# The general path's weight loads, issued from GpSimd's queue in place of ACT's

## The chip, the cores and the metric

One core of a Trainium2 chip runs the whole kernel. The metric is the device time of one execution in microseconds (us); lower is better. The core has five engines with a queue of instructions each: TensorE (PE; PEld is its weight load), VectorE (DVE), ScalarE (ACT), GpSimd (POOL) and SyncE (SP). Each queue runs in its own order, and a queue waits for another through semaphores.

## The reference, cut to what matters

Two layers, each a mixer (pooling, a recurrent scan in both directions, attention, an output product, LayerNorm) and then a mixture of experts over 256 tokens. Of the 32 experts every token uses two, and the result goes through a LayerNorm:

```python
def expert_block(args):
    xb, e = args
    h = jax.nn.silu(xb @ w_gate[e]) * (xb @ w_up[e])
    return h @ w_down[e]
...
x = layer_norm(DEEPNORM_ALPHA * x + m, ln2_g[l], ln2_b[l])
```

The weights of all 32 experts are read in each layer, whatever the tokens choose: three matrices of 1024 x 512 in float32 for each.

## The kernel before, in words

**The fast path.** Each layer's experts run in NQ = 8 quarters of four experts (the loop over q in `experts`). Every expert has CH = 32 slots for tokens. A quarter gathers its tokens by products with a one-hot matrix (`gather_steps`, the helper at L168), scales them into the tiles xg on ACT (`gathered`, L1230), multiplies by the gate and up weights (`gate_up`; all its products are issued by the helper at L172 and go by the tiles pg and pu), transposes the result, multiplies by the down weights (`down`, tile py) and adds the gated result to the tokens (`combine`, tile pc).

**The weights.** A quarter has 24 weight slabs of 1 MiB (128 partitions x 2048 floats), 192 in a layer. They are loaded by SP alone, in order, by the generator `loads` at L1039, into a ring of RING = 22 slabs. The program is unrolled, and each time a quarter takes a slab, the next load is put into SP's queue, so the queue runs FLIGHT = 22 slabs ahead. A load must wait until the slab that it writes over has been read by TensorE.

**Completion semaphores.** The framework counts the loads of SP's and ACT's queues on eight semaphores that the two queues share, taken in turn. Before each load SP waits until the load eight places earlier has landed (the EVENT_SEMAPHORE instructions at L1039), so at most eight are in flight.

**The general path.** An expert that is chosen by more than 32 tokens needs further passes. After the second quarter (q equal to OVQ = 1) `overflow` reads the largest slot count on all five queues (`values_load`, L1304) and branches (`tc.If(cv > CH)`, L1305). Inside are two nested loops at run time, which load weights in pieces of 256 KiB into the tiles ow on ACT's queue (`piece`, L1317): 24 x 4 = 96 loads in one pass of the body. POOL computes nothing inside.

When the branch isn't taken, each queue runs the else side that the framework adds. It brings every semaphore that the body would have counted up to the value that the body would have left, so that what follows the branch can wait for one value. In the program of the kernel before, the else side holds one such instruction for ACT, for PE and for DVE, none for POOL, and eight for SP, one for each shared semaphore. Each first waits for the count that stands for all loads issued so far, and then adds the body's share:

```text
else side, SP, for each of the eight shared DMA semaphores:
    wait until the semaphore is at least 192, then add 192      (96 loads / 8 semaphores x 16)
```

The xg tiles behind the branch lie in the same ring of buffers as ow (tag "r", 9 buffers), so the first ACT instruction behind the branch (L1230) waits for these semaphores. Of the 24 slabs of a quarter, 22 can lie in the ring.

Of the kernel before, what the change touches and what calls it, by code (L numbers as in the profile page):

```python
# [68 lines left out]
def tile_encoder(ctx: ExitStack, tc: tile.TileContext, x_tok, x_t, w_a0, w_a1, w_b0, w_b1, w_o,  # L69
                 cols, ln_rows, consts, rcnt, e_w, out):  # L70
    nc = tc.nc
# [137 lines left out]
    def s2(shape, name):  # L209
        return mp.tile(shape, F32, name=name, tag="r", bufs=RB)  # L210
# [987 lines left out]
    def one_hot(slots):  # L1198
        oh = s1([128, 2, 4, CH], "OH")
        io = iota[:, 0:CH].rearrange("p (a b s) -> p a b s", a=1, b=1).to_broadcast([128, 2, 4, CH])  # L1200
        V.tensor_tensor(oh, io, slots.rearrange("p i (a s) -> p i a s", s=1).to_broadcast([128, 2, 4, CH]), op=OP.is_equal)  # L1201
        return oh
# [6 lines left out]
    def experts(l, x1, xr, oh0, exps, gates, count, wts, feed):  # L1209
# [24 lines left out]
        def gather(oh):  # L1234
            banks = None
            for banks in gather_steps(oh):
                pass
            return gathered(banks)

        def gated(oh, gts):  # L1240
            V.tensor_tensor(oh, oh, gts.rearrange("p i (a s) -> p i a s", s=1).to_broadcast([128, 2, 4, CH]), op=OP.mult)

        def slots_t(oh):
            pt = bank("oht")
            for i in range(2):
                PE.transpose(pt[:, 128 * i:128 * i + 128], oh[:, i].rearrange("p a s -> p (a s)"), ident)  # L1246
            oht = s1([128, T], "OHT")
            A.copy(oht, pt[:, 0:T])
            return oht

        def gate_up(xg, w, between=lambda n: None):
            ps_g, ps_u = bankc("pg"), bankc("pu")
            for m, ps in enumerate((ps_g, ps_u)):
                for k in range(8):
                    wk_ = w(8 * m + k)
                    for a in range(4):
                        mm(ps[quad(a)], xg[k // 4][:, k % 4, CH * a:CH * a + CH], wk_(a), start=(k == 0), stop=(k == 7))
                    between(8 * m + k)
            h_ = s2([128, 512], "h")
            A.activation(h_, ps_g, AF.Silu)  # L1260
            V.tensor_mul(h_, h_, ps_u)  # L1261
            return h_

        def hid_t(h_):
            h3 = h_.rearrange("p (c k) -> p k c", k=4)
            pt = bank("pht")
            for k in range(4):
                PE.transpose(pt[:, 128 * k:128 * k + 128], h3[:, k], ident)
            hT = s2([128, 4, 128], "hT")
            V.tensor_copy(hT, pt.rearrange("p (k s) -> p k s", k=4))  # L1270
            return hT

        def down(hT, w, between=lambda n: None, keep=None):
            y = []
            if keep is not None:
                keep["y"] = y
            for hf in range(2):
                py = bank("py")
                for k in range(4):
                    wk_ = w(16 + 4 * hf + k)  # L1280
                    for a in range(4):
                        mm(py[quad(a)], hT[:, k, CH * a:CH * a + CH], wk_(a), start=(k == 0), stop=(k == 3))
                    between(4 * hf + k)
                y_ = s2([128, 512], "y")
                A.copy(y_, py)  # L1285
                y.append(y_)
            return y
# [7 lines left out]
        def combine_all(oht, y):  # L1295
            for hf in range(2):
                for i in range(2):
                    combine(oht, y, hf, i)
# [4 lines left out]
        def overflow():  # L1303
            cv = nc.values_load(cnt[0:1, 0:1], min_val=0, max_val=T)  # L1304
            with tc.If(cv > CH):  # L1305
                ovf = s2([128, 3, 2, NE], "ovf")
                sl, gt, tmp = (ovf[:, m] for m in range(3))
                V.tensor_copy(sl, slot)
                V.tensor_copy(gt, gate)
                with tc.For_i(0, T // CH - 1, 1):  # L1310
                    V.tensor_scalar(sl, sl, float(CH), None, op0=OP.subtract)
                    with tc.For_i(0, NQ, 1) as qi:
                        def wt(n):
                            def piece(a):
                                t_ = s2([128, 512], "ow")
                                v_ = e_w[l, :, n][bass.ds(qi, 1)].rearrange("o p n -> (o p) n")
                                nc.scalar.dma_start(out=t_, in_=v_[:, 512 * a:512 * a + 512])  # L1317
                                return t_
                            return piece

                        oh = one_hot(sl[:, :, 0:4])
                        xg = gather(oh)
                        gated(oh, gt[:, :, 0:4])
                        oht = slots_t(oh)
                        combine_all(oht, down(hid_t(gate_up(xg, wt)), wt))
                        for z in (sl, gt):
                            V.tensor_copy(tmp[:, :, 0:NE - 4], z[:, :, 4:NE])
                            V.tensor_copy(tmp[:, :, NE - 4:NE], z[:, :, 0:4])
                            V.tensor_copy(z, tmp)
# [307 lines left out]
```

## Time and profile before

| | us |
|---|---|
| median of 3 runs | 1278.93 |
| lowest, highest | 1277.48, 1283.57 |
| profiled execution, its own time | 1281.9 |
| span of the profiled execution | 1280.1 |

The span runs from the first to the last instruction of one profiled execution; its own time lies 1.8 us above the span and 3.0 us above the median of the runs. TensorE is busy for 77% of the span, DVE for 26%, ACT for 19%, POOL for 7%; the mean granted clock of TensorE is 0.871. The core moves 438.67 MB at a mean of 343 GB/s. SP's loads go over the hardware queue q1, ACT's over q10.

In the rows below a name such as SPq or ACTq is the queue of that engine, that is, instructions that its sequencer handles alone (branches, semaphores, DMA issues).

### The profile page before, as it was taken

The page shows a single profiled execution, that of the slowest core. Times are in us where ns is not written, and L with a number is a line of the kernel's source. Part 1 is how long each engine was busy: PE and PEld are TensorE (multiplying, and loading weights), DVE is VectorE, ACT ScalarE, POOL GpSimd, SP SyncE. Part 2 cuts the span into 40 slices and gives each one's busy share as a digit, 9 for nine tenths or more (in the row PEclk, how much of TensorE's full clock was granted, in tenths as well). Part 3 has the DMA queues.
Part 4 walks back from the last instruction along what each step waited for, and adds up shares of the span by engine and source line. Part 5 has one row for each costly group of instructions (what it writes and reads, how often), then busy time and mean ns, then how long its engine had stood idle before and what let it go on. Part 6 is the DMA issues. An engine that isn't in the chain of part 4 may idle for free. (4 is left out here: it accounts for less than half of the span.)

```text
span 1280.1 us, 18020 instructions
## 1 busy us (share of the span) xinstructions
PE 985.9 (77%) x7571; PEld 480.6 (38%) x7571; DVE 335.9 (26%) x774; ACT 239.2 (19%) x554; POOL 94.0 (7%) x137
## 2 busy tenths in 40 slices
PE   8988998933997777776698979989239977777753
PEld 7755763220441212221286657632214422223100
DVE  5937632110100001010368286411001000010103
ACT  5326422001110101010252353220011101010000
POOL 1143000000000000000101451000000000000002
PEclk9979999965998888886799789999669988888887
DMA  9413789998999999999940227999989999999994
GB/s 373 165 37 131 307 327 418 420 418 331 420 419 419 420 420 420 420 419 420 417 170 9 89 79 320 365 420 420 419 330 420 419 420 420 419 420 420 419 420 188
DMA packets 63452, 438.67 MB, mean 343 GB/s; under 512 B 7040, under 2 KB 7296, under 8 KB 11520
## 3 DMA queue, kind: packets, MB, share of 16 engines
q1 hardware_dynamic: 62784, 436.61, 83.1%
q8 instruction: 64, 1.05, 0.3%
q10 hardware_dynamic: 576, 0.79, 0.2%
q14 instruction: 28, 0.23, 0.0%
HBM read 436.32 MB, written 1.05 MB: 342 GB/s over the span
## 5 line engine op out<-in xcount | busy, mean ns | idle before, releaser
L172 PE MATMUL pg<-w,xg 128*32 128x512 f32 x1024 | 143.4, 658 | 120.3 <-ACT xg L1230 73.1
L172 PE MATMUL pu<-w,xg 128*32 128x512 f32 x1024 | 157.0, 700 | 39.2 <-DMA w<-in_e_w_dram 39.1
L172 PE MATMUL py<-w,hT 128*32 128x512 f32 x1024 | 146.0, 697 | 53.4 <-DMA w<-in_e_w_dram 42.4
L1261 DVE TENSOR_TENSOR h<-h,pu 128x512 f32<-128x512 f32 x16 | 11.0, 688 | 422.5 <-PE pu L172 218.3
L172 PEld LDWEIGHTS pg<-w,xg 128*32 128x32 f32 x1024 | 25.3, 114 | 215.8 <-DMA w<-in_e_w_dram 87.2
L1230 ACT ACTIVATE xg<-xg,lnc 128x128 f32<-128x128 f32 x112 | 41.8, 457 | 326.5 <-PE xg L168 219.6
L1293 DVE TENSOR_TENSOR xr<-xr,pc 128x512 f32<-128x512 f32 x56 | 38.5, 688 | 242.2 <-PE pc L172 242.2
L168 PEld LDWEIGHTS xg<-OH,xr 128*128 128x128 f32 x256 | 65.0, 331 | 61.9 <-issue 55.5
L168 PEld LDWEIGHTS xg<-OH,x 128*128 128x128 f32 x256 | 65.0, 331 | 59.4 <-issue 53.0
L172 PEld LDWEIGHTS py<-w,hT 128*32 128x32 f32 x1024 | 29.1, 117 | 154.1 <-DMA w<-in_e_w_dram 83.4
L168 PE MATMUL xg<-OH,xr 128*128 128x128 f32 x256 | 75.7, 433 | 12.0 <-DVE OH L1201 4.0
L168 PE MATMUL xg<-OH,x 128*128 128x128 f32 x256 | 75.6, 429 | 11.0 <-PEq L1305 4.1
L172 PE MATMUL pc<-y,OHT 128*128 128x512 f32 x128 | 70.0, 641 | 1.4 <-ACT y L1285 1.4
L1285 ACT COPY y<-py 128x512 f32<-128x512 f32 x32 | 18.7, 585 | 242.8 <-PE py L172 242.8
L231 POOL TENSOR_TENSOR w<-w 128x512 fp32r<-128x512 f32 (+1 forms) x20 | 25.2, 1265 | 497.4 <-ACT w L230 497.4
L172 PEld LDWEIGHTS pu<-w,xg 128*32 128x32 f32 x1024 | 23.6, 116 | 97.7 <-DMA w<-in_e_w_dram 80.5
L269 PE MATMUL wo<-w 128*128 128x512 f32 x192 | 46.5, 398 | 0.0
L196 POOL TENSOR_TENSOR lnmv<-lnmv,eps 128x1 f32<-128x1 f32 x8 | 4.8, 602 | 524.5 <-DVE lnmv L195 524.5
L172 PEld LDWEIGHTS pc<-y,OHT 128*128 128x128 f32 x128 | 20.1, 190 | 54.4 <-issue 46.0
L269 PEld LDWEIGHTS wo<-w 128*128 128x128 f32 x192 | 35.6, 188 | 9.1 <-issue 1.6
L230 ACT CAST w<-w 128x512 fp32r<-128x512 f32 (+1 forms) x64 | 36.6, 602 | 8.8 <-DMA w<-in_w_a_dram 4.8
L168 PE MATMUL pq<-w 128*128 128x512 f32 x64 | 38.0, 740 | 0.0
(328 smaller groups left out, 1064.8 us busy)
## 6 DMA issues: line engine op xcount, KB each, us to landing
w<-in_e_w_dram SPq DMA_DIRECT2D x384, 1024.0 KB, 19.9
w<-in_w_b_dram SPq DMA_DIRECT2D x8, 1024.0 KB, 18.7
w<-in_w_o_dram SPq DMA_DIRECT2D x8, 1024.0 KB, 19.9
w<-in_w_a_dram SPq DMA_DIRECT2D x4, 1024.0 KB, 13.5
lnr<-in_ln_rows_dram SPq DMA_DIRECT2D x12, 256.0 KB, 14.5
w<-in_w_a_dram SPq DMA_DIRECT2D x4, 448.0 KB, 6.3
w<-in_w_a_dram SPq DMA_DIRECT2D x2, 896.0 KB, 12.4
w<-in_cols_dram SPq DMA_DIRECT2D x2, 790.0 KB, 10.5
```

What stands on the lines that cost most here:

```text
L168: PE.matmul(ps, lhsT=lhsT, rhs=rhs, start=start, stop=True, skip_group_check=True)
L172: PE.matmul(ps, lhsT=lhsT, rhs=rhs, start=start, stop=stop)
L196: G.tensor_tensor(mv[:, 3:4], mv[:, 2:3], eps[:, 4:5], op=OP.pow)
L230: A.copy(hi, src)
L231: (V, G)[LOW[m]].tensor_tensor(lo, src, hi.bitcast(F32), op=OP.subtract)
L269: PE.matmul(ps, lhsT=l_[a], rhs=r_[b], start=first and n == 0, stop=last, skip_group_check=True)
L1230: A.activation(t_[:, k], ps[:, k], AF.Identity, scale=lnc["g1"][:, m:m + 1], bias=lnc["b1"][:, m:m + 1])
L1261: V.tensor_mul(h_, h_, ps_u)
L1285: A.copy(y_, py)
L1293: V.tensor_add(o_, o_, ps)
```

## The change

The loads of the general path are issued by GpSimd's queue. Nothing else differs: tiles, sizes, order and the branch are those of before.

```diff
@@ -1314,7 +1314,7 @@
                             def piece(a):
                                 t_ = s2([128, 512], "ow")
                                 v_ = e_w[l, :, n][bass.ds(qi, 1)].rearrange("o p n -> (o p) n")
-                                nc.scalar.dma_start(out=t_, in_=v_[:, 512 * a:512 * a + 512])
+                                nc.gpsimd.dma_start(out=t_, in_=v_[:, 512 * a:512 * a + 512])
                                 return t_
                             return piece
```

## Rows read from the trace of the kernel before

**Rows 1.** Page, part 2: GB/s moved in 40 slices of 32 us.
```profile
GB/s 373 165 37 131 307 327 418 420 418 331 420 419 419 420 420 420 420 419 420 417 170 9 89 79 320 365 420 420 419 330 420 419 420 420 419 420 420 419 420 188
```

**Rows 2.** The chain that ended last: start us, us, what.
```profile
947.95 0.47 ACT xg L1230
...
956.50 12.64 DMA w<-in_e_w_dram
...
969.20 19.90 DMA w<-in_e_w_dram
...
1250.07 12.58 DMA w<-in_e_w_dram
```

**Rows 3.** DMA issues by line and queue: KB each, us to landing.
```profile
q10 hardware_dynamic: 576, 0.79, 0.2%
...
w<-in_rcnt_dram ACTq DMA_DIRECT2D x2, 256.0 KB, 2.7
...
out_dram<-xr ACTq DMA_DIRECT2D x1, 160.0 KB, 2.3
out_dram<-xr ACTq DMA_DIRECT2D x1, 96.0 KB, 1.7
```

**Rows 4.** Line L1305, the branch: duration ns min/median/max, first and last start us.
```profile
L1305 SPq EVENT_SEMAPHORE  x16: 17/17/17, 291.8 to 947.8; - x16
L1305 POOLq COMPARE_BRANCH  x2: 45/45/45, 218.2 to 856.1; - x2
L1305 ACTq COMPARE_BRANCH  x2: 45/50/54, 256.1 to 894.1; - x2
L1305 PEldq COMPARE_BRANCH  x2: 6012/6050/6088, 256.8 to 894.8; - x2
...
L1305 ACTq EVENT_SEMAPHORE  x2: 17/17/17, 261.4 to 899.4; - x2
L1305 PEldq EVENT_SEMAPHORE  x2: 51/51/51, 262.9 to 900.8; - x2
L1305 SPq COMPARE_BRANCH  x2: 50/52/53, 290.5 to 928.8; - x2
```

**Rows 5.** The same line from 255 to 320 us, the first layer's branch alone.
```profile
L1305 SPq EVENT_SEMAPHORE  x8: 17/17/17, 291.8 to 309.2; - x8
```

**Rows 6.** Waits, who for whom: us in total, times, longest.
```profile
ACT xg L1230 <- SPq L1305: 106.9, 2, 53.7
...
SPq L1039 <- DMA w<-in_e_w_dram: 584.0, 282, 3.2
...
SPq L1305 <- SPq L1305: 37.5, 14, 6.4
```

**Rows 7.** Timeline, first layer, around the branch.
```profile
255.38 3.70 PE L172 MATMUL pc<-y,OHT 128*128 128x512 f32 x8
...
263.15 3.69 PE L168 MATMUL xg<-OH,x 128*128 128x128 f32 x14 [4.07 <-PEq L1305]
268.48 4.44 PE L168 MATMUL xg<-OH,x 128*128 128x128 f32 x18 [1.64 <-issue]
...
309.33 2.90 ACT L1230 ACTIVATE xg<-xg,lnc 128x128 f32<-128x128 f32 x8 [53.23 <-SPq L1305]
```

**Rows 8.** Windows: us; busy by engine (count); granted clock, DMA share, GB/s.
```profile
290.00:304.00 14.00, 0.00 (x0) 0.00 (x0) 0.00 (x0) 0.00 (x0) 0.00 (x0) 0.50 1.01 420
304.00:318.00 14.00, 8.16 (x54) 2.16 (x58) 0.00 (x0) 3.27 (x9) 0.00 (x0) 0.63 0.56 217
...
942.00:956.00 14.00, 7.54 (x50) 1.99 (x54) 0.00 (x0) 3.27 (x9) 0.00 (x0) 0.62 0.56 218
...
332.00:640.00 308.00, 235.37 (x1282) 77.88 (x1278) 35.58 (x65) 34.74 (x77) 4.02 (x6) 0.86 1.01 419
...
956.00:1262.00 306.00, 237.15 (x1340) 77.16 (x1330) 27.69 (x45) 26.90 (x62) 0.00 (x0) 0.89 1.01 417
```

**Rows 9.** POOL's groups from 150 to 640 us: busy, mean ns, idle before.
```profile
L231 POOL TENSOR_TENSOR w<-w 128x448 fp32r<-128x448 f32 x2 | 2.2, 1128 | 462.1 <-ACT w L230 462.1
```

## The prediction

> **What bounds the kernel now.** I began with the chain that ended last. From 956.50 us to 1262.65 us it is one load of expert weights after another [rows 2]: eight loads of 1 MiB in 19.90 us, or 2.49 us each, 421 GB/s. The slices of the page say the same of both expert stages: 417 to 420 GB/s, slice after slice, and two holes among them, 331 (288 to 320 us) and 330 (928 to 960 us) [rows 1]. So an expert stage lasts as long as its weights take to arrive, and only time in which the loads stand still can be won there. What follows either stage (the last quarter's end, the second layer's mixer, the final LayerNorm) begins when its last slab has landed, and a microsecond won in the stream is one won in the time.
>
> What makes the holes? The chain begins at 947.95 us with ACT's xg at L1230 [rows 2], and the waits say for whom that instruction waited: for SP's queue at L1305, the branch, two times, 106.9 us in all [rows 6]. In the first layer TensorE ends its second quarter at 259.08 us (255.38 + 3.70), starts the next gather at 263.15, ends it at 272.92 (268.48 + 4.44), and then has nothing until ACT, whose xg it needs, starts at 309.33 after 53.23 us of idleness [rows 7]. From 290 to 304 us no engine computes, and the granted clock of TensorE is 0.50, the lower of its levels (1.2 GHz); the loads run on at 420 GB/s [rows 8].
>
> SP reaches the branch late: at 290.5 us, where ACT and PE come at 256.1 and 256.8 [rows 4]. Its queue is in order, and at each slab it waits for the load eight places earlier (282 waits, 584.0 us [rows 6]). Then come its eight semaphore instructions of the else side, the first at 291.8 and the last at 309.2 us [rows 5]: 17.4 us, some seven landings at 2.49 us. By its own waits, 37.5 us in 14 steps over both layers [rows 6], SP stays there until everything it issued has landed. All 22 slabs of the ring are then full, no load is in flight, and none may start before TensorE has read a slab. ACT is released at that moment, 0.13 us after the last semaphore. The ramp from there is the hole: 217 GB/s for the 14 us from 304 to 318, and 218 for those from 942 to 956, where 420 is the rate before [rows 8].
>
> **The change, part by part.** What the edit moves are the 96 loads of the branch's body. Do they run? ACT's hardware queue moved 0.79 MB in the whole execution [rows 3]: the two loads of 256 KB in the mixers and the two stores of 160 and 96 KB come to 768 KB, which is all of it. No load of ow ran, in either layer, and with the same inputs none will. So the loads cost nothing before and after, and the price of an issue from GpSimd doesn't enter. A rule of the Trainium skill speaks against such a move (DMA: Bandwidth & Descriptors, Issuing engine by pattern): simple loads belong on Sync's or ACT's queues, whose descriptors come from hardware, and are generally slower from GpSimd. No run of the general path lies in this trace, so nothing here bears on that rule, and with no load executed the sum by it is the same as without it.
>
> What is left is the branch not taken. The else side counts up the semaphores that the body uses: one in each layer for ACT and one for PE (and one for DVE), none for POOL, which computes nothing in the body, and eight for SP [rows 4]. I read the pattern as: only what the body touches. Once the loads leave ACT's queue, the body touches none of the eight semaphores that SP's weight loads count on. SP then has nothing to wait for at the branch: 16 semaphore instructions and the drain behind them go, 17.4 us in the first layer and the like in the second.
>
> Added: loads of a queue that has none elsewhere need semaphores of their own, so the else side must count those, on POOL or on SP. If on POOL, they run at its branch, at 218.2 and 856.1 us [rows 4], long before ACT needs them: nothing is in flight on them, so there is nothing to wait for, and at 17 ns each (SP's row) eight take 0.14 us. POOL's body grows as ACT's had been, and its branch of 45 ns may come to cost what PE's does over a long body, 6.05 us [rows 4]. Both ends are free: POOL next has work some 410 us later (it is idle for 462.1 us before that [rows 9]), and ACT, which needs them at 273, would still have its semaphores by about 225 us. If that cover were gone, 6.1 us per layer would be the price. The Trainium skill (Runtime: NRT & Kernel Launch, Instruction fetch mechanics) says that a taken branch past the prefetched instructions waits for a fetch; the 6.05 us beside 45 ns on the short bodies agree with it.
>
> If on SP, they run at 290.5 us plus 0.14 us; ACT is then released at 290.7 in place of 309.3.
>
> Who is late next? In the first case only the gather is ahead of ACT: it ends at 272.92 us [rows 7], and with 0.47 us for ACT's first piece [rows 2] the first gate product starts at about 273.5 us. The ring then holds the slabs that landed since 256, some seven at 2.49 us. In the second case it starts at 291. Either way the first slab is read within 1 to 2 us, SP's next load, which waits for the load eight places earlier at about 292, finds its buffer free, and the stream never empties. TensorE can follow: from 956 to 1262 us it keeps up with the loads with 237 of 306 us busy, and from 332 to 640 with 235 of 308 [rows 8]. So the loads remain the bound.
>
> **The sum.** First layer: 14 us x (420 - 217) / 420 = 6.77 us. Second layer: 14 us x (420 - 218) / 420 = 6.73 us. Together 13.5 us. Nothing is added on the path. By the profiled execution's own time: 1281.9 - 13.5 = 1268.4 us. That execution lies 3.0 us above the median of the runs, 1278.93; against the median I forecast 1265.4 us, 1.06% less. The bounds: the hole's edge windows are 14 us wide, and a GB/s either way in the rate is 0.07 us in both holes together, so the size stands to some 0.3 us; the median of three runs that spread from 1277.48 to 1283.57 us is the larger doubt, about 2 us to either side. The likeliest case alone therefore spans 1262 to 1269.
>
> **The rivals.**
>
> *SP drains all the same: no change.* The else side could settle all DMA semaphores whether the body uses them or not. Then ACT waits until 309.3 as before, and the time stays at 1278.9. For it: SP's eight cover every semaphore that its queue shares. Against it: POOL's missing instruction [rows 4], and that ACT, PE and DVE settle one each, their own. The Trainium skill's section "Issuing engines are not separate DMA queues" (DMA: Bandwidth & Descriptors) would also have it so: another issuing queue saves only the sequencer's issue time, and here no such load is issued. The rows put the cost elsewhere, in a wait on shared counts. I give this 9 in 100.
>
> *Half of it.* One layer's hole stays, or a smaller hole opens in each, because something else in the branch is still late for ACT. A hole opens once the release comes after about 309.3 - 6.8 = 302.5 us, and grows by a microsecond for each later one. One layer's worth gives 1278.9 - 6.7 = 1272.2; 5 in 100.
>
> *POOL's side is slow: slower.* The release is now POOL's, and its else side or its branch could take far longer than any row shows. It decides nothing up to 302.5 us, 84 us behind POOL's branch at 218.2; at 309.3, 91 us behind, all is as before; to be slower by 0.5% over both layers (6.4 us) it would take 94 us behind each branch. The nearest rows are 17 ns for a semaphore and 6.05 us for a branch over a long body, so 94 us would be fifteen such fetches one after another. At 100 us the time would be 1278.9 + 2 x (218.2 + 100 - 309.3) = 1296.7. I give it 3 in 100.
>
> *More than the hole.* TensorE stands at half its clock while it waits and then has 22 slabs to work off; without that, the quarters behind the branch run smoother. But they are bound by loads at 417 to 419 GB/s [rows 8], with nothing left to win: 1260 or less, 3 in 100.
>
> **How the numbers follow.** The likeliest case has 80 in 100, and its time is the forecast, 1265.4 us. A change of 0.5% is 6.4 us, about what a measurement of this kernel can tell from none. Faster by more: 80 + 3 and most of the half case, 4, so 0.87. Within: the rival of no change, 9, and 1 of the half case, 0.10. Slower: 0.03. The range leaves out the case of no change and the slow one, 12 in 100, and the far gain; it reaches from 1261 us, past the runs' spread, to 1272.5 us, over the half case.
>
> **What would show it.** SP has no semaphore instruction at L1305, where it had 16. If POOL has them instead, they stand right behind 218 us, and ACT's xg at L1230 waits for TensorE's gather alone and starts at about 273 us in the first layer; if SP has them, at about 291. The row of ACT waiting for SP's branch, 106.9 us, is gone. From 290 to 330 us the loads run at 419 to 420 GB/s, and the slices of 331 and 330 read 417 to 420. SP's next load behind the branch starts near 292. The stage behind each branch is as long as before, only earlier. The forecast is wrong if SP still settles its eight, if ACT still starts after 302 us, or if a second hole opens later in the stream.

## The result, and the profile after

The changed kernel took 1265.38 us (median of 4 runs, 1264.30 to 1266.36) beside 1279.56 us for the kernel before (4 runs, 1277.48 to 1283.57): a ratio of 0.9896, with a 95% interval of 0.9875 to 0.9917. The forecast was 1265.4 us. Run again later, beside the kernel without the branch, the same kernel took 1266.02 us against 1277.83, 0.9895 [0.9870, 0.9921]. The ratios here and below stand as the comparison gave them; they are not the quotients of the two medians, and differ from these by up to 0.3%. The span of the profiled execution fell from 1280.1 to 1262.6 us.

The rate of the loads over the span, in 40 slices, answers to [rows 1]:

```profile
GB/s 369 168 44 135 298 328 413 418 418 418 420 420 419 419 419 420 419 419 420 417 188 9 97 74 321 373 418 420 417 419 419 420 420 420 419 420 421 419 419 180
```

The two holes of 331 and 330 GB/s are gone; every full slice of the two expert stages now reads 417 to 421. The branch's line answers to [rows 4] (duration in ns min/median/max, first and last start):

```profile
L1305 POOLq EVENT_SEMAPHORE  x8: 17/43/43, 222.9 to 850.8; - x8
L1305 POOLq COMPARE_BRANCH  x2: 45/48/50, 217.5 to 845.3; - x2
L1305 POOLq INC_SWDGE_SEM  x2: 167/172/177, 223.3 to 850.9; - x2
L1305 ACTq COMPARE_BRANCH  x2: 45/45/45, 254.4 to 883.3; - x2
L1305 ACTq EVENT_SEMAPHORE  x2: 17/17/17, 254.9 to 883.7; - x2
L1305 PEldq COMPARE_BRANCH  x2: 6132/6140/6148, 255.1 to 884.0; - x2
...
L1305 SPq COMPARE_BRANCH  x2: 50/52/53, 290.0 to 917.8; - x2
```

SP's sixteen semaphore instructions are no longer there. POOL has eight, four at each branch, and is through with them by 223.5 us in the first layer, 47 us before ACT needs them. SP still reaches the branch at 290.0 us, as late as before, but nothing waits for it now. The timeline around the branch, as in [rows 7]:

```profile
253.72 3.70 PE L172 MATMUL pc<-y,OHT 128*128 128x512 f32 x8
...
267.14 5.39 PE L168 MATMUL xg<-OH,x 128*128 128x128 f32 x22 [2.87 <-issue]
...
270.65 1.50 ACT L1230 ACTIVATE xg<-xg,lnc 128x128 f32<-128x128 f32 x4 [16.21 <-PE xg L168]
272.46 4.72 PE L172 MATMUL pg<-w,xg 128*32 128x512 f32 x40
```

ACT waits for the gather, its own data, and starts at 270.65 us, where it had started at 309.33. Of all waits of ACT at L1230 only that one is left, where [rows 6] had two waits for SP:

```profile
ACT xg L1230 <- PE xg L168: 273.1, 28, 23.8
```

The windows of [rows 8] show the hole itself filled (length, busy time by engine with counts, granted clock, DMA share, GB/s):

```profile
290.00:304.00 14.00, 11.72 (x70) 6.84 (x74) 1.71 (x3) 3.00 (x8) 0.00 (x0) 0.88 1.01 419
304.00:318.00 14.00, 8.76 (x53) 1.32 (x46) 0.00 (x0) 1.17 (x2) 0.00 (x0) 0.76 1.01 418
...
942.00:956.00 14.00, 11.99 (x58) 2.25 (x50) 3.09 (x5) 0.96 (x2) 0.00 (x0) 0.88 1.01 421
```

Where 217 and 218 GB/s stood, 418 and 421 stand. ACT's hardware queue moved what it had moved before, 0.79 MB, and no load of ow appears:

```profile
q10 hardware_dynamic: 576, 0.79, 0.2%
```

The spans differ by 17.5 us, the medians by 14.2. The profiles place the difference, by POOL's first work on the second layer, before and after:

```profile
628.92 2.22 POOL L231 TENSOR_TENSOR w<-w 128x448 fp32r<-128x448 f32 x2 [462.10 <-ACT w L230]
622.00 2.22 POOL L231 TENSOR_TENSOR w<-w 128x448 fp32r<-128x448 f32 x2 [455.90 <-DVE lnmv L195]
```

That work (the group of [rows 9]) starts at 622.00 us where it had started at 628.92: 6.9 us, the first hole. POOL reaches the second branch 10.8 us earlier (845.3 against 856.1), so the mixer between ran 3.9 us shorter in this execution. From there to the end another 6.7 us are won, the second hole. The diff touches nothing in that mixer; the differences of the medians, 14.2 us and, in the second set, 11.8, lie to either side of the 13.6 us (6.9 and 6.7) of the two holes.

### The profile page after: what moved, and what is told of

The parts are those of the page before. It is cut to its first block, busy times and chain, and to the rows that moved or that the text cites. A ratio compares the mean times of both kernels' runs of the same rounds, so it can differ in the third digit from the quotient of the medians.

```text
span 1262.6 us, 18036 instructions
## 1 busy us (share of the span) xinstructions
PE 998.6 (79%) x7571; PEld 476.2 (38%) x7571; DVE 336.3 (27%) x774; ACT 239.4 (19%) x554; POOL 94.1 (7%) x137
## 5 line engine op out<-in xcount | busy, mean ns | idle before, releaser
L172 PE MATMUL py<-w,hT 128*32 128x512 f32 x1024 | 154.0, 716 | 71.7 <-DMA w<-in_e_w_dram 60.7
L172 PE MATMUL pu<-w,xg 128*32 128x512 f32 x1024 | 160.6, 715 | 57.1 <-DMA w<-in_e_w_dram 57.1
L1230 ACT ACTIVATE xg<-xg,lnc 128x128 f32<-128x128 f32 x112 | 42.1, 455 | 273.1 <-PE xg L168 273.1
L168 PE MATMUL xg<-OH,x 128*128 128x128 f32 x256 | 75.3, 430 | 12.3 <-PEq L1305 4.1
L168 PE MATMUL pq<-w 128*128 128x512 f32 x64 | 34.8, 688 | 0.0
```

The source lines that it names most:

```text
L168: PE.matmul(ps, lhsT=lhsT, rhs=rhs, start=start, stop=True, skip_group_check=True)
L172: PE.matmul(ps, lhsT=lhsT, rhs=rhs, start=start, stop=stop)
L1230: A.activation(t_[:, k], ps[:, k], AF.Identity, scale=lnc["g1"][:, m:m + 1], bias=lnc["b1"][:, m:m + 1])
```

## The experiments

Each kernel is compared with the kernel before on the same chip, by ratio; that kernel's median was 1277.3 to 1278.5 us there. The figures in brackets are 95% intervals.

**The loads on SP's queue.** Off ACT's queue too, but still on the shared semaphores.

```diff
-                                nc.scalar.dma_start(out=t_, in_=v_[:, 512 * a:512 * a + 512])
+                                nc.sync.dma_start(out=t_, in_=v_[:, 512 * a:512 * a + 512])
```

> The general path's loads issued from SP's queue, so off ACT's queue but still counted on the eight semaphores that SP's weight loads use. Shared-semaphore theory: SP still settles its eight semaphores behind the branch and drains, ACT is released at about 309 us, both holes of 6.7 us stay, 1277 to 1282 us. Rival (the 96 loads in ACT's stream are what delays ACT, by the fetch of its code): ACT's stream is as short as in the changed kernel, so 1264 to 1268 us.

Measured: 1277.43 us, a ratio of 0.9999 [0.9973, 1.0025], no change, as expected. The branch's line and the waits of this run:

```profile
L1305 SPq EVENT_SEMAPHORE  x16: 17/17/17, 293.7 to 939.1; - x16
...
L1305 ACTq COMPARE_BRANCH  x2: 45/45/45, 253.9 to 884.8; - x2
L1305 ACTq EVENT_SEMAPHORE  x2: 17/17/17, 254.0 to 885.3; - x2
```

```profile
ACT xg L1230 <- SPq L1305: 107.4, 2, 54.2
```

ACT's stream is as short as in the changed kernel, and its own semaphore comes 0.1 us behind its branch in the first layer. Yet SP settles its sixteen, and ACT waits 107.4 us for them as before. What counts is not whether the loads leave ACT but which semaphores they are counted on.

**GpSimd's queue in the first layer alone.**

```diff
-                                nc.scalar.dma_start(out=t_, in_=v_[:, 512 * a:512 * a + 512])
+                                (nc.gpsimd, nc.scalar)[l].dma_start(out=t_, in_=v_[:, 512 * a:512 * a + 512])
```

> GpSimd's queue in the first layer's branch, ACT's in the second's. Shared-semaphore theory: the first hole goes, the second stays, half the gain: 1279.5 - 7 = 1272.5 us, 1271 to 1274; eight semaphore instructions on SP at the branch, all behind 900 us. Rival (one cause for the whole program, such as a queue set up or a better start): all or nothing, 1265 or 1279 us.

Measured: 1270.57 us, 0.9948 [0.9925, 0.9972], half the gain; the median lies just under the 1271 to 1274 us expected. The page's slices, and SP's semaphores at the branch:

```profile
GB/s 371 172 37 132 311 324 410 419 419 418 419 421 420 419 419 421 420 419 420 417 150 9 102 68 375 375 420 419 420 334 421 418 420 420 419 420 421 420 420 177
```

```profile
L1305 SPq EVENT_SEMAPHORE  x8: 17/17/17, 922.8 to 935.4; - x8
```

The first hole is gone (418 in the tenth slice) and the second stands (334). SP's eight semaphores all start at 922.8 us or later, at the second layer's branch. Each branch costs by itself, and the gain is no matter of the whole program.

**A body without loads.**

```diff
-                                nc.scalar.dma_start(out=t_, in_=v_[:, 512 * a:512 * a + 512])
+                                G.memset(t_, 0.0)
```

> The general path's body has no loads at all; its weight tiles are filled with zeros on GpSimd (the body doesn't run with these inputs). Shared-semaphore theory: no DMA semaphore to settle, time as in the changed kernel, 1264 to 1267 us. Rival (GpSimd's queue itself gives something, or its counting costs something): a difference of more than 0.3% from 1265.4 us either way.

Measured: 1265.01 us, 0.9926 [0.9902, 0.9949]. Its slices:

```profile
GB/s 372 166 44 135 304 316 418 418 418 419 419 419 420 420 420 420 419 420 419 418 196 10 102 69 358 373 419 419 417 420 420 420 420 419 420 419 419 421 419 149
```

Both holes are gone (419 and 420 in the tenth and the thirtieth slice), and no semaphore of SP's is left at the branch: taking the loads off the shared semaphores is enough to close the holes. Whether GpSimd's queue gives or costs a few microseconds of its own is not settled. The median is that of the changed kernel within 0.4 us; the ratio is 0.3% above the changed kernel's 0.9896, and the two intervals overlap from 0.9902 to 0.9917.

**No branch.** The call of `overflow` is left out, with the general path in it.

```diff
                 combine_all(*done)
                 done = None
-                overflow()
```

> The general path and its branch are left out, so only experts with up to 32 tokens are computed rightly (these inputs have no others). Shared-semaphore theory: with the drain gone the branch costs nothing, since PE's 6 us of fetching are hidden behind loads: 1263 to 1267 us, no gain over the changed kernel. Rival (the branch still costs its fetches and register loads on the path, some 6 us per layer): 1252 to 1256 us.

Measured: 1268.37 us, 0.9932 [0.9910, 0.9954], above the 1263 to 1267 us expected. That is 3.0 us above the changed kernel's first median, which stood beside another set of runs, so both were run again on one chip.

> The changed kernel itself, beside the kernel before and the one without the branch on one chip: about 0.989 of the kernel before, 13.5 us less (theory: both holes gone).

> The kernel without the general path and its branch, again, on the same chip as the changed kernel. Theory (the branch costs nothing once the drain is gone): within 0.3% of the changed kernel, 4 us. Rival (its fetches cost 6 us per layer): 12 us less. Second rival (the branch gives something, as the median of 1268.4 us in its first run may hint): 3 us or more above the changed kernel.

Measured: the changed kernel 1266.02 us, 0.9895 [0.9870, 0.9921]; without the branch 1268.46 us, 0.9926 [0.9903, 0.9948]. The intervals overlap, so no difference is shown. That leaving the branch out wins 12 us is ruled out: with the drain gone, its 6.1 us of PE and its register loads lie wholly behind the stream of weights. Whether the branch gives back a few microseconds, as both medians without it might suggest, stays open.

**Eight loads held back.** The kernel before, drain and all, but the last eight slabs that SP would have asked for ahead of the branch are asked for right behind it.

```diff
+HOLD = 8
...
-                wts.extend(v_ for v_ in (next(feed, None),) if v_ is not None)
+                if not (cut_ and n >= 24 - HOLD):
+                    wts.extend(v_ for v_ in (next(feed, None),) if v_ is not None)
...
                 overflow()
+                wts.extend(next(feed) for _ in range(HOLD))
```

> The kernel before (loads on ACT's queue, drain kept), but eight of SP's weight loads that stood ahead of the branch are put right behind it, so that at the drain's end eight slabs of the ring are free. The theory's hole has two parts: nothing in flight, and nothing that may be asked for until PE reads a slab. Here the second part is gone: ACT is released near 290 us and SP issues eight loads at once, so the hole shrinks to the delay of a first load, 1.5 to 3 us per layer: 1269 to 1273 us. Rival (the drain alone makes the hole): 6.7 us per layer as before, 1278 to 1281 us. Second rival (only the late release matters): no hole, 1264 to 1267 us.

Measured: 1271.41 us, 0.9946 [0.9924, 0.9969]. Its timeline, and its rate from 280 to 300 us in 40 slices of half a microsecond (line numbers are one higher in this kernel):

```profile
288.45 2.90 ACT L1231 ACTIVATE xg<-xg,lnc 128x128 f32<-128x128 f32 x8 [33.44 <-SPq L1306]
288.45 5.13 SPq L1040 DMA_DIRECT2D w<-in_e_w_dram  x9
```

```profile
GB/s 361 459 393 410 492 344 459 410 410 475 279 279 180 147 115 16 0 0 115 147 16 492 410 393 459 377 475 426 377 492 393 360 475 393 442 459 344 508 442 344
```

SP reaches the branch at 269.7 us here, with eight loads fewer ahead of it, and ACT is released 21 us earlier than in the kernel before; a hole remains all the same. The drain ends at 288.3 us, and SP issues at once, without waiting for TensorE. The loads fade over 2.5 us before it, stand still for about 1.5, and are back at the full rate 2 us after. Its windows give the size:

```profile
276.00:290.00 14.00, 1.04 (x8) 0.39 (x12) 0.00 (x0) 1.55 (x5) 0.00 (x0) 0.50 0.81 317
290.00:304.00 14.00, 14.00 (x104) 4.34 (x94) 0.00 (x0) 2.32 (x6) 0.00 (x0) 0.89 0.98 410
...
914.00:928.00 14.00, 8.28 (x54) 2.16 (x58) 0.00 (x0) 3.28 (x9) 0.00 (x0) 0.62 0.76 304
```

14 us x (420 - 317) / 420 + 14 us x (420 - 410) / 420 = 3.8 us in the first layer, and 14 us x (420 - 304) / 420 = 3.9 us in the second, where 1.5 to 3 were expected. So the hole of 6.75 us has two parts: 3.8 us of draining and restarting, measured here, and by difference 2.9 us of waiting for TensorE to free a slab. The sum over both layers falls from 13.5 to 7.7 us; the time fell by 1277.29 - 1271.41 = 5.9.

**GpSimd made late.** The changed kernel, with 120, 150 or 180 powers of one column on GpSimd ahead of its branch, begun when the count is there.

```diff
+            dly = tiny([128, 2], "dly")
+            G.memset(dly, 1.0)
+            G.tensor_copy(dly[0:1, 1:2], cnf)
+            for _ in range(120):
+                G.tensor_tensor(dly[:, 0:1], dly[:, 0:1], eps[:, 4:5], op=OP.pow)
             cv = nc.values_load(cnt[0:1, 0:1], min_val=0, max_val=T)
```

> The changed kernel with 120 one-column powers on GpSimd ahead of its branch in each layer, begun when the count is known (about 217 us), 0.56 us each: GpSimd's else side, and with it ACT, comes at about 217 + 67 + 6 = 290 us. By the prediction's threshold (a hole opens when ACT is released after 302.5 us) no cost: 1264 to 1267 us, although PE waits 18 us longer per layer. Rival (each microsecond of PE's waiting costs): about 2 x 18 us more, 1300 us.

> As the one with 120, with 150: ACT released at about 307 us. By the threshold 302.5 us a hole of about 4.5 us per layer: 1274 us, 1268 to 1281 by how long one power takes. Rival (no cost as long as the release is before the end of SP's loads at 309 us): 1264 to 1267 us.

> As the one with 120, with 180: ACT released at about 324 us, hole 21 us per layer, 1265.4 + 43 = 1308 us, 1295 to 1320; between the run with 150 and this one the time grows by two microseconds (one per layer) for each microsecond of later release. The slower rival of the prediction, made on purpose: GpSimd's side slow. A theory in which GpSimd's branch is off the path would give 1264 to 1267 us here too.

Measured: 1265.56 us, 0.9916 [0.9886, 0.9947], with 120; 1288.16 us, 1.0100 [1.0068, 1.0133], with 150; 1327.29 us, 1.0408 [1.0375, 1.0441], with 180. The expected times were 1264 to 1267, 1274 (1268 to 1281) and 1308 us (1295 to 1320): the first held, the other two came out too low. A power took 0.55 us, but one followed the other only every 0.63 us, so the releases came later than expected. Where ACT starts in the first layer, and the windows behind it, for 120:

```profile
299.32 2.90 ACT L1230 ACTIVATE xg<-xg,lnc 128x128 f32<-128x128 f32 x8 [43.27 <-remote]
```

```profile
288.00:302.00 14.00, 2.17 (x12) 0.60 (x16) 0.00 (x0) 2.68 (x8) 4.89 (x9) 0.50 1.01 419
302.00:316.00 14.00, 14.00 (x98) 4.77 (x90) 0.00 (x0) 1.19 (x3) 0.00 (x0) 0.92 1.02 418
```

for 150:

```profile
311.60 2.90 ACT L1230 ACTIVATE xg<-xg,lnc 128x128 f32<-128x128 f32 x8 [60.36 <-remote]
```

```profile
288.00:302.00 14.00, 0.00 (x0) 0.00 (x0) 0.00 (x0) 0.00 (x0) 12.27 (x23) 0.50 0.98 406
302.00:316.00 14.00, 3.89 (x20) 0.99 (x24) 0.00 (x0) 2.90 (x8) 5.60 (x11) 0.50 0.09 19
```

and for 180:

```profile
329.17 2.90 ACT L1230 ACTIVATE xg<-xg,lnc 128x128 f32<-128x128 f32 x8 [78.91 <-remote]
```

```profile
288.00:302.00 14.00, 0.00 (x0) 0.00 (x0) 0.00 (x0) 0.00 (x0) 12.27 (x23) 0.50 0.93 386
302.00:316.00 14.00, 0.00 (x0) 0.00 (x0) 0.00 (x0) 0.00 (x0) 12.22 (x23) 0.50 0.00 1
316.00:330.00 14.00, 0.32 (x4) 0.20 (x8) 0.00 (x0) 0.83 (x3) 8.77 (x16) 0.50 0.00 1
330.00:344.00 14.00, 14.00 (x100) 4.46 (x96) 0.00 (x0) 3.04 (x8) 0.00 (x0) 0.87 0.81 325
```

("remote" is what the trace writes for a release that it can't name; it comes 0.3 to 0.4 us behind the start of POOL's INC_SWDGE_SEM, at 299.0, 311.2 and 328.8 us.) With 120, TensorE's next quarter starts at 299.8 us, 27 us later than in the changed kernel, and the loads run on at 419 and 418 GB/s: the wait costs nothing. The holes of the first layer, summed over such windows as 14 us x (420 - rate) / 420, of the rows shown, are 0, 13.8 and 32.2 us. SP reached the branch at 290.5 us with 120, but at 284.6 and 284.7 with 150 and 180, some 4 to 5 us of which had been won in the first mixer of those profiled executions (the first xg on ACT at 209.9 and 208.6 us beside 213.8); the hole is therefore told against SP's branch:

| first layer | ACT's start behind SP's branch, us | hole, us | difference, us |
|---|---|---|---|
| with 120 | 8.8 | 0 | |
| kernel before | 18.8 | 6.8 | 12.0 |
| with 150 | 27.0 | 13.8 | 13.2 |
| with 180 | 44.5 | 32.2 | 12.3 |

The stream bears a release up to some 12 to 13 us behind SP's branch, and each later microsecond costs one. The second layer, read in the same way, gives 12.4 us for the kernel before, and 13.1 and 12.9 us with 150 and 180. The time with 150 was given as 1274 us and missed: the release came 4.6 us later than worked out and SP's loads ran out 6 us earlier. With 180 the release was 5 us later than worked out, beside the same earlier end of the loads.

## Why the prediction was right

**What bounds it.** That only time in which the loads stand still can be won held in both directions: 27 us more of TensorE's waiting cost nothing in the run with 120, and longer holes cost about their length: both layers' holes sum to 26.4 us with 150 powers and 62.8 us with 180, and the medians lie 22.6 and 61.7 us above the run with 120, which has none.

**What the edit moves.** That no load of ow runs held: ACT's queue moved 0.79 MB before and after, and no run of this study took the general path. What its loads cost when issued from GpSimd stays open; the rule of the Trainium skill that speaks against it (DMA: Bandwidth & Descriptors, Issuing engine by pattern) was not tried.

**Where the hole lies.** The prediction called the ramp behind ACT's release the hole. The rate of the kernel before from 285 to 325 us, in 40 slices of one microsecond, shows it on both sides:

```profile
GB/s 410 418 410 434 426 418 410 410 451 401 426 401 418 442 418 418 410 418 434 418 377 229 115 25 0 0 16 49 205 410 418 385 385 393 418 426 434 426 418 418
```

The loads fade from 305 us on, and about 2.5 of the hole's 6.8 us are lost before ACT starts at 309.33. The window from 304 to 318 us holds both sides, so the sum was right all the same.

**What is left of the branch.** The pattern read from [rows 4], that the else side settles only what the body touches, was the step on which all hung. It is shown by the runs with the loads on SP (still settled, still 1277 us) and without loads (nothing to settle, 1265 us). The rival of no change fell with it. What the section "Issuing engines are not separate DMA queues" of the Trainium skill (DMA: Bandwidth & Descriptors) says of issuing queues therefore did not forecast the time: the issuing queue mattered through the semaphores that its loads are counted on. That ACT waits for these because xg shares its ring of buffers with ow is read from the program; xg in a ring of its own was not tried.

**What is added.** The settling went to POOL, as the first case had it, with four semaphores at each branch where eight were reckoned, and one further instruction of 0.17 us. The fetch that POOL was to pay came too, if not inside the branch: the branch instruction stayed at 45 to 50 ns, and the first semaphore follows 5.4 us behind it (217.5 to 222.9). ACT's rows before had shown as much, 5.3 us behind a branch of 45 to 54 ns [rows 4]; the prediction, which went by PE's row, did not use them.

**Who is late next.** The gather, as forecast; ACT started at 270.65 us where 273 was reckoned, because its first half of xg is ready before the gather ends.

**The sum.** 13.5 us were predicted; the medians differ by 14.2, and with the second set by 1277.83 - 1266.02 = 11.8. The interval of the first ratio, 0.83% to 1.25%, holds the 1.06%. One layer's change alone gave 0.9948, about half of it. That 1265.4 us and the first median agree within 0.1 us is luck: the kernel before stood at 1278.93 us in the forecast and at 1279.56 us in the comparison, and the two sets put the gain 2.4 us apart.

**The slower rival.** Its mechanism is real and its threshold was right: 302.5 us was 12.0 us behind SP's branch, and the runs give 12 to 13. It did not happen because POOL was done 47 us ahead.

## What to carry to other kernels

Code that never runs can cost time through its bookkeeping: at a branch, look at which semaphores the untaken side has to settle, and who else counts on them. Keep a rare path's transfers off the semaphores of the stream that bounds the kernel; any way of doing so (another queue's semaphores, or no transfer at all) gave the same time here within the noise (1265.38 and 1265.01 us). Where a drain can't be avoided, hold back as many loads as there are in flight, so that they can be issued without waiting for a buffer: that alone won 5.9 us of 13.5.

## What the runs showed of the hardware that was not expected

A wait behind the branch went with the long body, from queue to queue. With the loads on ACT its own semaphore came 5.3 us behind its branch (256.1 to 261.4 us [rows 4]); with the loads on GpSimd that gap was 0.5 us on ACT and 5.4 us on POOL. With the loads on SP it was 0.1 us on ACT, and on SP 5.4 us (288.3 to 293.7) where it had been 1.3 [rows 4]; but SP's semaphores also wait for landings, and in the second layer its gap was 6.6 us beside 6.4 in the kernel before. Loads are not what it takes: in the run without loads, whose body fills the tiles on GpSimd, POOL's gap was 0.5 us in the first layer and 5.3 us in the second, and why they differ is not known. The Trainium skill (Runtime: NRT & Kernel Launch, Instruction fetch mechanics) tells of such a wait, for a fetch, behind a branch that leaves what has been fetched ahead; the gaps on ACT and POOL agree with it. More direct are the runs with 150 and 180 powers, in which no weight load was moving at POOL's branch. From the branch to POOL's first semaphore (308.4 to 310.9 us with 150, first layer) one packet of 0.01 MB moved in all, on the instruction queue q14. The same holds at the other three such branches. Whose packet it was the trace does not say. The gap was 2.5 to 2.8 us there, and 5.1 to 5.2 us with 120, where the weight loads ran at 418 and 419 GB/s: beside the full stream the wait was about twice as long.

Draining and restarting the loads has a price even where no buffer is waited for: in the run with eight loads held back, 3.8 us of the full rate went between the fading of the old loads and the full rate of the new ones, though SP issued the first 0.2 us after the last semaphore (288.3 to 288.5 us).
